# Expert queries one head at a time, the first head routed at once, later routings placed by the stream of gathered rows

## The chip, the cores and the metric

The kernel runs on one core of a Trainium2 chip (trn2). It was timed as device microseconds of whole executions: the median of three runs is 3098.87 us (3098.61 to 3099.56). The profile is of one further execution.

The engines are named as the profile has them: PE (TensorE, with PEld for its weight loads), DVE (VectorE), ACT (ScalarE), POOL (GpSimd) and SP (SyncE). Each runs its own instructions in order and waits for the others by semaphores. PE is TensorE's busy row, PEclk the clock granted to it, as a share of full speed.

## The reference

The model has two blocks of layers over 256 tokens of width 2048: a gated linear recurrence, attention with forget gates, and then a layer that mixes a recurrent branch with sparse attention. The change touches only the last part, a mixture of very many small experts. `x` has 256 rows; there are 8 heads, 128 x 128 experts and 16 experts per head and token.

```python
q = (xf @ wq).reshape(t, PEER_HEADS, PEER_QDIM)          # 256 columns per head
s1 = jnp.einsum('thd,kd->thk', q[..., :half], keys1)
s2 = jnp.einsum('thd,kd->thk', q[..., half:], keys2)
v1, i1 = lax.top_k(s1, PEER_TOPK)
v2, i2 = lax.top_k(s2, PEER_TOPK)
cand_s = (v1[..., :, None] + v2[..., None, :]).reshape(t, PEER_HEADS, -1)
cand_i = (i1[..., :, None] * PEER_KEYS + i2[..., None, :]).reshape(t, PEER_HEADS, -1)
top_s, pos = lax.top_k(cand_s, PEER_TOPK)
expert = jnp.take_along_axis(cand_i, pos, axis=-1).reshape(t, -1)
gate = jax.nn.softmax(top_s.astype(jnp.float32), axis=-1)
...
z = jnp.einsum('cd,ced->ce', xc, u[ec])
act = jax.nn.gelu(z, approximate=False) * gc
return jnp.einsum('ce,ced->cd', act, v[ec])
```

Each token reads 128 rows of `u` and 128 rows of `v`, each of 2048 float32. A residual sum and a final norm follow.

## The kernel before

**The weight loop.** All dense products go through one loop, `run`. It takes a list of steps; each step has 1024 columns per partition of weights (two steps are one load of 1 MB on SP's queue, into one of three `raw` buffers). The weights are split into a high part `hi` (a copy on ACT) and a low part `lo` (a subtraction on DVE), three steps ahead of PE, and PE multiplies 24 times per step. After the matmuls of a step the loop calls `pump`, which advances every open task by one piece, up to its next `yield`. So the order of instructions on each engine is fixed when the program is built: a task that yields lets the next step's `hi`, `lo` and matmuls go in between.

**The last 32 steps** make the experts' queries. Four units (`unit_B`, names `eq`) of 512 columns, that is two heads, have 8 steps each. When a unit ends, its task `e_query(n)` waits until the norm of the stream is known (`stE.done`; the row `stE_R` holds the factor of each token), scales the accumulator into `eq`, multiplies it with the two sets of keys on PE (`esc`), copies the scores (`es`), and calls `e_route` for token tile 0 and, when all four pairs have had theirs, for tile 1.

**Routing** (`e_route`) is DVE work: for two heads at once, four searches for the 16 highest of 128 scores (`top16`: MAX8, FIND_INDEX8, MATCH_REPLACE8, MAX8, FIND_INDEX8), 50 candidate pairs by nine additions and nine multiply-adds, a search over the 50 for each head, a comparison with a row of numbers to find the experts' numbers (three instructions over 128 x 800), a cast into `idx` (line 1349), and the softmax into `gate`. It yields some nine times.

**The stream** (`e_stream`) is a task too. It gathers rows: for each of 16 groups (8 heads x 2 token tiles) and each of 16 places, one gather of 128 rows from `e_u` (U) and one from `e_v` (V), 512 in all, each with an indirect DMA on POOL's queue (line 1363). U rows are multiplied with the token's row and summed on DVE (line 1393, 128 x 2048, "the product" below). V rows are scaled and summed on PE, as a matmul with a diagonal matrix `dg` (line 1411; ACT makes `dg`); in the last two groups every second V is added on DVE instead. Each piece of the task handles one row buffer and issues gathers for the free ones. There are three buffers (`rows_l`, and `rows_h` twice) until all queries are done; then `wide_rows` adds six (three `rows_w` in the place of `raw`, `rows_xh`, and `rows_xl` twice). U and V alternate once V may start, which is also when all queries are done.

In short, the DVE queue holds, in the order in which the tasks are advanced: `lo` of the weights, products of rows, pieces of routing, and query products.

Of the kernel before, what the change touches and what calls it, by code (L numbers as in the profile page):

```python
# [62 lines left out]
def tile_model(ctx: ExitStack, tc: tile.TileContext, x, xT, par, a_in, a_out, kv_in, kv_f, b_in, b_out,  # L63
# [313 lines left out]
    def unit_B(src, xt, cb, name, nk=KT):  # L377
# [850 lines left out]
    Ee = {"tk": 0, "r1": 0, "q": 0, "routed": [False] * NG16}  # L1228
# [24 lines left out]
    def e_query(n):  # L1253

        def f(acc):
            while not hasattr(stE, "done"):
                yield
            q = w4(f"eq{n}", (P, 4, T))
            tt_(q, acc, stE.R[:, None, :].to_broadcast([P, 4, T]), OP.mult)
            yield  # L1260
            yield
            ps = side_tile("esc").rearrange("p a (j k) -> p (a j) k", k=EK)
            for j in range(4):
                for t in range(TT):
# [17 lines left out]
            Ee["r1"] += 1  # L1282
# [18 lines left out]
    def e_route(n, tt, s):  # L1301

        NH = 2
        buf = w4(f"route{n}_{tt}")
        at = [0]

        def part(*shape):
# [3 lines left out]
            if len(shape) == 2:  # L1311
                return o.rearrange("p (a b) -> p a b", b=shape[1])
            return o.rearrange("p (a b c) -> p a b c", b=shape[1], c=shape[2])

        v, xi, ii = part(NH, 2, TK), part(NH, 2, TK), part(NH, 2, TK).bitcast(U32)
        cs, ci = part(NH, NCAND), part(NH, NCAND)
        tv, tp, pf, px = part(NH, TK), part(NH, TK).bitcast(U32), part(NH, TK), part(NH, TK)
        sm = part(NH, 1)
        for h in range(NH):
            for a_ in range(2):  # L1320
                top16(v[:, h, a_, :], ii[:, h, a_, :], s[:, (h * 2 + a_) * TT + tt, :])
            yield
# [13 lines left out]
        for r in range(NH):  # L1336
            top16(tv[:, r, :], tp[:, r, :], cs[:, r, :])
# [191 lines left out]
```

## Time and profile before

| what | value |
|---|---|
| median of three runs | 3098.87 us |
| the profiled execution, whole / its span | 3099.93 us / 3098.2 us |
| PE, DVE, ACT, POOL busy | 2677.9, 1912.0, 997.9, 780.9 us |
| queue of the gathers | 73728 packets, 536.90 MB |
| queue of the weights and other loads | 43920 packets, 298.73 MB |
| chain that ended last, by engine | PE 59%, DMA 25%, DVE 9%, issue 5%, POOL 2% |

The page gives the span in 40 slices of 77.5 us; there the bytes moved per slice and the busy shares of the engines show which stage runs. The first 22 slices are the dense layers, the gathers run from about slice 22 to the end. A share of busy time over the whole span mixes these stages, so the argument is made in the stage that the change touches.

### The profile page before, as it was taken

The page shows a single profiled execution, that of the slowest core. Times are in us where ns is not written, and L with a number is a line of the kernel's source. Part 1 is how long each engine was busy: PE and PEld are TensorE (multiplying, and loading weights), DVE is VectorE, ACT ScalarE, POOL GpSimd, SP SyncE. Part 2 cuts the span into 40 slices and gives each one's busy share as a digit, 9 for nine tenths or more (in the row PEclk, how much of TensorE's full clock was granted, in tenths as well). Part 3 has the DMA queues.
Part 4 walks back from the last instruction along what each step waited for, and adds up shares of the span by engine and source line. Part 5 has one row for each costly group of instructions (what it writes and reads, how often), then busy time and mean ns, then how long its engine had stood idle before and what let it go on. Part 6 is the DMA issues. An engine that isn't in the chain of part 4 may idle for free.

```text
span 3098.2 us, 34719 instructions
## 1 busy us (share of the span) xinstructions
PE 2677.9 (86%) x13236; PEld 1957.5 (63%) x13236; DVE 1912.0 (62%) x2840; ACT 997.9 (32%) x1545; POOL 780.9 (25%) x612
## 2 busy tenths in 40 slices
PE   8999999999999999999999747677777777777765
PEld 8999888888888899999989723222222222222222
DVE  7867665656665558566565899744444454444465
ACT  6545544555554445455454200100000000000000
POOL 0412110000000000000000143555555555554553
PEclk9999999999999999999999878899999999999988
DMA  7444445444445444444455689899999999999998
GB/s 260 150 149 151 167 160 178 164 162 177 167 154 193 175 164 171 161 173 170 171 177 192 231 316 358 358 421 422 421 422 421 421 422 422 421 421 422 422 421 332
DMA packets 118534, 841.13 MB, mean 271 GB/s; under 512 B 13152, under 2 KB 13536, under 8 KB 17376
## 3 DMA queue, kind: packets, MB, share of 16 engines
q0 software_dynamic: 73728, 536.90, 42.1%
q1 hardware_dynamic: 43920, 298.73, 27.0%
q10 hardware_dynamic: 720, 3.28, 0.3%
q8 instruction: 104, 1.70, 0.2%
q14 instruction: 62, 0.51, 0.0%
HBM read 836.77 MB, written 2.10 MB: 271 GB/s over the span
## 4 chain that ended last, share of the span: by engine, by line
PE 59%; DMA 25%; DVE 9%; issue 5%; POOL 2%; ACT 0%; POOLq 0%; DVEq 0%; ACTq 0%
DMA rows_w<-in_e_v_dram,slots 7%; DMA rows_xl<-in_e_v_dram,slots 5%; DMA rows_h<-in_e_v_dram,slots 5%; PE vacc L1411 5%; DMA rows_l<-in_e_v_dram,slots 3%; DMA rows_xh<-in_e_v_dram,slots 2%; DVE rows_h L1393 1%; PE S L554 1%; DVE eq L86 1%; PE aq L391 1%; PE aq L393 1%; PE aq L392 1%; PE az L391 1%; PE da L391 1%; PE az L392 1%
## 5 line engine op out<-in xcount | busy, mean ns | idle before, releaser
L86 DVE TENSOR_TENSOR lo<-raw,hi 128x1024 fp32r<-128x1024 f32 x424 | 520.3, 1232 | 301.7 <-PE dx L393 36.3
L102 ACT ACTIVATE hi<-raw 128x1024 fp32r<-128x1024 f32 x424 | 447.1, 1058 | 542.0 <-PE az L392 59.1
L1411 PE MATMUL vacc<-rows_w,dg_ring 128*128 128x512 f32 x640 | 311.3, 632 | 139.3 <-DMA rows_w<-in_e_v_dram,slots 93.2
L1411 PEld LDWEIGHTS vacc<-rows_w,dg_ring 128*128 128x128 f32 x640 | 122.3, 201 | 327.5 <-issue 211.0
L1411 PE MATMUL vacc<-rows_h,dg_ring 128*128 128x512 f32 x424 | 200.8, 619 | 82.9 <-DMA rows_h<-in_e_v_dram,slots 57.3
L1411 PE MATMUL vacc<-rows_xl,dg_ring 128*128 128x512 f32 x432 | 204.7, 618 | 69.5 <-DMA rows_xl<-in_e_v_dram,slots 62.6
L247 POOL TENSOR_TENSOR rq_y<-rq_m,mhalf 128x8 f32<-128x8 f32 (+2 forms) x24 | 31.6, 1317 | 888.2 <-DVE rq_m L95 881.6
L98 DVE SCALAR_TENSOR_TENSOR lo<-raw,prm,hi 128x512 fp32r<-128x512 f32 x256 | 178.8, 748 | 105.0 <-issue 62.0
L102 ACT ACTIVATE dg_ring<-ident,slots 128x128 f32<-128x128 f32 x240 | 83.6, 392 | 444.4 <-PE vacc L1411 444.2
L102 ACT ACTIVATE hi<-raw,prm 128x512 fp32r<-128x512 f32 x256 | 170.7, 717 | 120.8 <-PE bg L418 31.3
L1411 PEld LDWEIGHTS vacc<-rows_h,dg_ring 128*128 128x128 f32 x424 | 79.3, 196 | 203.6 <-issue 131.0
L1411 PEld LDWEIGHTS vacc<-rows_xl,dg_ring 128*128 128x128 f32 x432 | 80.8, 196 | 192.3 <-issue 145.2
L102 ACT ACTIVATE slots<-slots 128x16 f32<-128x16 f32 x16 | 3.4, 216 | 591.4 <-DVE rows_h L1393 142.9
L1393 DVE SCALAR_TENSOR_TENSOR rows_w<-rows_w,stE_r,rows_xh 128x2048 f32<-128x2048 f32 x43 | 101.1, 2351 | 106.4 <-DMA rows_w<-in_e_u_dram,slots 106.2
L1363 POOL DMA_INDIRECT rows_w<-in_e_u_dram,slots x80 | 125.9, 1574 | 155.8 <-PE vacc L1411 153.0
L1393 DVE SCALAR_TENSOR_TENSOR rows_w<-rows_w,stE_r,rows_l 128x2048 f32<-128x2048 f32 x37 | 86.9, 2349 | 74.7 <-DMA rows_w<-in_e_u_dram,slots 74.7
L1411 PE MATMUL vacc<-rows_l,dg_ring 128*128 128x512 f32 x208 | 98.2, 616 | 38.4 <-DMA rows_l<-in_e_v_dram,slots 26.1
L1411 PE MATMUL vacc<-rows_xh,dg_ring 128*128 128x512 f32 x216 | 101.8, 615 | 31.1 <-DMA rows_xh<-in_e_v_dram,slots 28.1
L1363 POOL DMA_INDIRECT rows_h<-in_e_u_dram,slots x64 | 95.1, 1485 | 132.5 <-PE vacc L1411 89.6
L1393 DVE SCALAR_TENSOR_TENSOR rows_xl<-rows_xl,stE_r,rows_xh 128x2048 f32<-128x2048 f32 x29 | 68.2, 2351 | 74.0 <-DMA rows_xl<-in_e_u_dram,slots 73.9
L1393 DVE SCALAR_TENSOR_TENSOR rows_h<-rows_h,stE_r,rows_l 128x2048 f32<-128x2048 f32 x36 | 84.5, 2347 | 46.6 <-DMA rows_h<-in_e_u_dram,slots 46.6
L1393 DVE SCALAR_TENSOR_TENSOR rows_h<-rows_h,stE_r,rows_xh 128x2048 f32<-128x2048 f32 x28 | 65.8, 2351 | 66.6 <-DMA rows_h<-in_e_u_dram,slots 66.5
(482 smaller groups left out, 7287.5 us busy)
## 6 DMA issues: line engine op xcount, KB each, us to landing
raw<-in_d_in_dram SPq DMA_DIRECT2D x76, 1024.0 KB, 4.8
raw<-in_a_in_dram SPq DMA_DIRECT2D x63, 1024.0 KB, 4.8
raw<-in_kv_in_dram SPq DMA_DIRECT2D x32, 1024.0 KB, 4.8
raw<-in_b_in_dram SPq DMA_DIRECT2D x32, 1024.0 KB, 4.7
raw<-in_a_out_dram SPq DMA_DIRECT2D x16, 1024.0 KB, 4.8
raw<-in_b_out_dram SPq DMA_DIRECT2D x16, 1024.0 KB, 4.8
raw<-in_d_out_dram SPq DMA_DIRECT2D x16, 1024.0 KB, 4.8
raw<-in_e_q_dram SPq DMA_DIRECT2D x16, 1024.0 KB, 4.8
```

Source lines behind the costliest of these rows:

```text
L86: V.tensor_tensor(o, a, b, op=op)
L98: V.scalar_tensor_tensor(o, a, s, b, op0=op0, op1=op1)
L102: S.activation(o, i, f, bias=bias, scale=scale)
L247: G.tensor_tensor(y, m, mhalf[:, :w], op=OP.pow)
L391: PE.matmul(a[:, j, :], lhsT=w_h, rhs=xt.h(kt), start=(kt == 0 and j % 2 == 0), stop=False)
L392: PE.matmul(a[:, j, :], lhsT=w_h, rhs=xt.l(kt), start=False, stop=False)
L393: PE.matmul(a[:, j, :], lhsT=w_l, rhs=xt.h(kt), start=False, stop=(kt == nk - 1 and j % 2 == 1))
L554: PE.matmul(o, lhsT=lhs[:, h, sl], rhs=r, start=True, stop=True)
L1363: G.indirect_dma_start(out=dst, out_offset=None, in_=table, in_offset=bass.IndirectOffsetOnAxis(ap=Ee["idx"][:, gi, k:k + 1], axis=0))
L1393: V.scalar_tensor_tensor(r, r, stE.r[:, t:t + 1], Ee["xw", t], op0=OP.mult, op1=OP.mult, accum_out=Ee["z"][:, gi, k:k + 1])
L1411: PE.matmul(accs[t][c // 2][:, c % 2, :], lhsT=dg, rhs=r[:, c * 512:(c + 1) * 512], start=(j == 0), stop=last)
```

## The change

Five things change, all in the experts' part.

- Units: 8 units of 256 columns (one head), 4 steps each, instead of 4 units of 512 columns with 8 steps (`unit_B2`). The weights are packed anew on the host; the steps, the matmuls and the bytes stay 32, 24 per step and 16 MB.
- The first head's query task has no `yield` between its product, its scores and its routing except one; the others keep theirs.
- `e_route` takes one head and one token tile. It has four pieces with a gap of a step between them. The searches are as before; the additions over the candidates have half the width, and as many instructions for one head as there were for two. The softmax takes its sum from ACT's exponential.
- A routing may start only when the ones ahead of it are done and the stream has issued U gathers to within 20 of its group's first one: `Ee["nu"]` is a count kept while the program is built.
- The scores of two heads share one tile `es`.

```diff
+        for i in range(4):
+            steps.append(Step(src(i // 2), mm(4 * i), ready=lambda k=i: xt.done() > k))
+        steps[-1].post = lambda: spawn(cb(box["acc"]))
...
-            q = w4(f"eq{n}", (P, 4, T))
-            tt_(q, acc, stE.R[:, None, :].to_broadcast([P, 4, T]), OP.mult)
-            yield
-            yield
-            ps = side_tile("esc").rearrange("p a (j k) -> p (a j) k", k=EK)
-            for j in range(4):
-                for t in range(TT):
...
+            q = w4(f"eq{h}", (P, 2, T))
+            tt_(q, acc, stE.R[:, None, :].to_broadcast([P, 2, T]), OP.mult)
+            yield
+            if h:
+                yield
+            ps = side_tile("esc")[:, 0, :].rearrange("p (t k) -> p t k", k=EK)
...
-            if Ee["q"] == 4:
+            if Ee["q"] == EH:
                 wide_rows()
-            yield
-            while Ee["tk"] < n:
-                yield
-            yield from e_route(n, 0, s)
-            Ee["tk"] += 1
-            while Ee["tk"] < 4 or Ee["r1"] < n:
-                yield
-            yield from e_route(n, 1, s)
-            Ee["r1"] += 1
+            for t in range(TT):
+                while Ee["route"] < t * EH + h or Ee["nu"] < (t * EH + h - 1) * TK - 4:
+                    yield
+                yield from e_route(h, t, s[:, 2 * t:2 * t + 2, :])
+                Ee["route"] += 1
...
+        for a_ in range(2):
+            top16(v[:, a_, :], ii[:, a_, :], s[:, a_, :])
+        yield
         V.tensor_copy(xi, ii)
...
+        top16(tv, tp, cs)
         V.tensor_copy(pf, tp)
...
+        V.tensor_reduce(px, eq, axis=AX.X, op=OP.add)
+        del eq
+        V.tensor_copy(Ee["idx"][:, gi, :], px)
+        Ee["routed"][gi] = True
+        yield
+        ts(tv, tv, tv[:, 0:1], OP.subtract)
+        act(tv, tv, AF.Exp, accum=sm)
+        yield
+        V.reciprocal(sm, sm)
+        ts(Ee["gate"][:, gi, :], tv, sm, OP.mult)
...
-                v_ok = Ee["q"] == 4 and nv < min(nu - nu % TK, len(us)) and \
+                v_ok = Ee["q"] == EH and nv < min(nu - nu % TK, len(us)) and \
...
                     it, nu = ("U",) + us[nu], nu + 1
+                    Ee["nu"] = nu
```

The order of instructions shows the change at three places. First ACT, from the row of the norm to the first scores; before, four `hi` copies of the steps after it stand between:

```order
L102 ACTIVATE hi_15225<-raw_15094 128x1024
L102 ACTIVATE stE_R<-Rps 128x256
L102 ACTIVATE hi_15258<-raw_15094 128x1024
L102 ACTIVATE hi_15288<-raw_15171 128x1024
L102 ACTIVATE hi_15319<-raw_15171 128x1024
L102 ACTIVATE hi_15356<-raw_15229 128x1024
L102 ACTIVATE es_15386<-esc 128x1024
```

Now one does, and the first `es` is half as wide:

```order
L102 ACTIVATE hi_15226<-raw_15094 128x1024
L102 ACTIVATE stE_R<-Rps 128x256
L102 ACTIVATE hi_15261<-raw_15094 128x1024
L102 ACTIVATE es_15294<-esc 128x512
L102 ACTIVATE hi_15309<-raw_15171 128x1024
L102 ACTIVATE hi_15365<-raw_15171 128x1024
```

So the first scores moved ahead by three weight steps of ACT's queue.

Second DVE, at the end of the first routing and the first products of rows (line 1393 before, 1410 now); `lo` are splits of weights. Before:

```order
L1345 TENSOR_REDUCE route_0_15416<-eq 128x16
L86 TENSOR_TENSOR lo_15626<-raw_15431,hi_15589 128x1024
L1349 CAST slots<-route_0_15416 128x32
L86 TENSOR_TENSOR lo_15664<-raw_15431,hi_15624 128x1024
L1393 SCALAR_TENSOR_TENSOR rows_l,slots<-rows_l,stE_r 128x2048
L1353 COPY route_0_15416<-route_0_15416 128x2
L86 TENSOR_TENSOR route_0_15416<-route_0_15416 128x32
L86 TENSOR_TENSOR lo_15703<-raw_15518,hi_15662 128x1024
L1393 SCALAR_TENSOR_TENSOR rows_h,slots<-rows_h,stE_r,rows_l 128x2048
```

Now, where the cast into `slots` follows its comparison at once:

```order
L1366 TENSOR_REDUCE route_0_15296<-eq 128x16
L1368 CAST slots<-route_0_15296 128x16
L86 TENSOR_TENSOR lo_15405<-raw_15171,hi_15365 128x1024
L1410 SCALAR_TENSOR_TENSOR rows_l,slots<-rows_l,stE_r 128x2048
L93 TENSOR_SCALAR route_0_15296<-route_0_15296 128x16
L86 TENSOR_TENSOR lo_15442<-raw_15230,hi_15403 128x1024
L1410 SCALAR_TENSOR_TENSOR rows_h,slots<-rows_h,stE_r,rows_l 128x2048
L1374 RECIPROCAL route_0_15296<-route_0_15296 128x1
```

Here the same sequence stands eight weight steps earlier: behind the first product 18 `lo` follow, before there were 10. Up to the first gather from `e_v` DVE has 25 products now and had 17.

Third POOL, where the first gather from `e_v` is issued and the buffers widen. Before, it is the 20th gather:

```order
L1363 DMA rows_l<-in_e_u_dram,slots 128x2048
L1363 DMA rows_h<-in_e_u_dram,slots 128x2048 x2
L1363 DMA rows_l<-in_e_u_dram,slots 128x2048
L1363 DMA rows_h<-in_e_v_dram,slots 128x2048
L1363 DMA rows_w_16244<-in_e_u_dram,slots 128x2048
L1363 DMA rows_w_16245<-in_e_v_dram,slots 128x2048
L1363 DMA rows_w_16246<-in_e_u_dram,slots 128x2048
```

Now it is the 28th, behind nine rounds of the three buffers:

```order
L1379 DMA rows_h<-in_e_u_dram,slots 128x2048 x2
L1379 DMA rows_l<-in_e_u_dram,slots 128x2048
L1379 DMA rows_h<-in_e_u_dram,slots 128x2048 x2
L1379 DMA rows_l<-in_e_v_dram,slots 128x2048
L1379 DMA rows_w_16224<-in_e_u_dram,slots 128x2048
L1379 DMA rows_w_16225<-in_e_v_dram,slots 128x2048
```

The order of U and V after that alternates in both; 19 V follow the last U before, 27 now. Behind the widening the routing of one head stands among 16 products each.

## Rows read from the trace of the kernel before

**Rows 1.** The page's slices of the span: GB/s in each of 40.

```profile
GB/s 260 150 149 151 167 160 178 164 162 177 167 154 193 175 164 171 161 173 170 171 177 192 231 316 358 358 421 422 421 422 421 421 422 422 421 421 422 422 421 332
```

**Rows 2.** Stretches: length, busy us of each engine, granted clock, DMA share, GB/s.

```profile
1720.00:1820.00 100.00, 55.64 (x381) 53.63 (x379) 90.11 (x212) 15.15 (x17) 22.93 (x20) 0.77 0.70 252
1820.00:2000.00 180.00, 119.74 (x240) 50.80 (x240) 164.05 (x475) 16.47 (x48) 85.30 (x66) 0.79 0.91 359
...
1840.00:1880.00 40.00, 29.63 (x63) 12.36 (x61) 38.52 (x133) 1.69 (x6) 18.75 (x15) 0.90 1.01 422
...
2000.00:3000.00 1000.00, 734.68 (x1578) 287.65 (x1576) 483.50 (x429) 72.16 (x214) 518.46 (x401) 0.99 1.01 422
3000.00:3080.00 80.00, 55.26 (x96) 21.42 (x96) 47.62 (x30) 3.98 (x11) 37.17 (x28) 0.83 1.00 415
```

**Rows 3.** Timeline of POOL (start, length, [idle before]): gathers 1, 20, 97, 512.

```profile
1725.52 1.21 POOL L1363 DMA_INDIRECT rows_l<-in_e_u_dram,slots  x1 [45.68 <-DVE slots L1349]
...
1819.31 1.45 POOL L1363 DMA_INDIRECT rows_h<-in_e_v_dram,slots  x1 [4.97 <-DVE rows_h L1393]
...
2024.03 1.66 POOL L1363 DMA_INDIRECT rows_xl<-in_e_u_dram,slots  x1 [2.06 <-PE vacc L1411]
...
3064.86 1.66 POOL L1363 DMA_INDIRECT rows_xl<-in_e_v_dram,slots  x1 [2.07 <-PE vacc L1411]
```

**Rows 4.** Timeline of ACT, DVE and PE: from the norm's row to the first scores.

```profile
1684.85 0.38 ACT L102 ACTIVATE stE_R<-Rps 128x256 f32<-128x256 f32 x1 [1.31 <-PE Rps L329]
...
1687.79 1.22 DVE L86 TENSOR_TENSOR eq<-eq,stE_R 128x1024 f32<-128x1024 f32 x1 [2.03 <-PE eq L393]
...
1693.28 1.95 PE L1265 MATMUL esc<-keys_iota,eq 128*128 128x128 f32 x16
...
1695.27 1.03 ACT L102 ACTIVATE es<-esc 128x1024 f32<-128x1024 f32 x1 [0.85 <-PE esc L1265]
```

**Rows 5.** Timeline of DVE: pieces of the first routing, of two heads.

```profile
1699.34 0.29 DVE L1295 MAX8 route<-es 128x8 f32<-128x128 f32 x1
...
1702.77 1.21 DVE L86 TENSOR_TENSOR lo<-raw,hi 128x1024 fp32r<-128x1024 f32 x1
...
1708.44 0.19 DVE L1323 CAST route<-route 128x64 f32<-128x64 uint32 x1
...
1710.02 1.22 DVE L86 TENSOR_TENSOR lo<-raw,hi 128x1024 fp32r<-128x1024 f32 x1
1711.15 0.21 DVE L1295 MAX8 route<-route 128x8 f32<-128x50 f32 x1
...
1713.78 1.21 DVE L86 TENSOR_TENSOR lo<-raw,hi 128x1024 fp32r<-128x1024 f32 x1
...
1715.11 0.99 DVE L86 TENSOR_TENSOR eq<-keys_iota,route 128x800 f32<-128x800 f32 x1
```

**Rows 6.** Timeline of DVE: the first products and what stands between them.

```profile
1733.10 2.35 DVE L1393 SCALAR_TENSOR_TENSOR rows_l<-rows_l,stE_r 128x2048 f32<-128x2048 f32 x1 [7.38 <-DMA rows_l<-in_e_u_dram,slots]
...
1735.37 0.17 DVE L1353 COPY route<-route 128x2 f32<-128x2 f32 x1
...
1735.68 1.22 DVE L86 TENSOR_TENSOR lo<-raw,hi 128x1024 fp32r<-128x1024 f32 x1
1736.82 2.35 DVE L1393 SCALAR_TENSOR_TENSOR rows_h<-rows_h,stE_r,rows_l 128x2048 f32<-128x2048 f32 x1
```

**Rows 7.** DMA issues: count, median us from issue to landing.

```profile
rows_w<-in_e_v_dram,slots POOLq DMA_INDIRECT x85, 18.8
...
rows_h<-in_e_u_dram,slots POOLq DMA_INDIRECT x64, 7.1
```

**Rows 8.** Waits of DVE from 2000 to 3080: us in total, times, longest.

```profile
DVE rows_w L1393 <- DMA rows_w<-in_e_u_dram,slots: 174.3, 66, 4.5
```

**Rows 9.** Timeline of DVE: the last V row.

```profile
3083.18 2.35 DVE L98 SCALAR_TENSOR_TENSOR xs<-rows_xl,slots,xs 128x2048 f32<-128x2048 f32 x1 [2.58 <-DMA rows_xl<-in_e_v_dram,slots]
```

**Rows 10.** Gathers of line 1363 from 2000: ns min/median/max, first and last start.

```profile
L1363 POOL DMA_INDIRECT rows_h<-in_e_v_dram,slots x50: 933/937/2806, 2007.4 to 3049.9; - x50
```

More of the change, by code (lines that the diff above doesn't have):

```diff
@@ L399, in unit_B, with unit_B2, mm, f @@
         steps[-1].post = lambda: spawn(cb(box["acc"].rearrange("p a (b t) -> p (a b) t", t=T)))
+        return steps
+    def unit_B2(src, xt, cb, name):
+        box = {}
+        steps = []
+        def mm(kt0):
+            def f(wh, wl):
+                if kt0 == 0:
+                    box["acc"] = acc_tile(name)[:, 0, :].rearrange("p (j t) -> p j t", t=T)
+                a = box["acc"]
+                h4, l4 = (w_.rearrange("p a (b n) -> p (a b) n", n=T) for w_ in (wh, wl))
+                for q in range(4):
+                    kt = kt0 + q
+                    for j in range(2):
+                        w_h, w_l = h4[:, q, j * P:(j + 1) * P], l4[:, q, j * P:(j + 1) * P]
+                        PE.matmul(a[:, j, :], lhsT=w_h, rhs=xt.h(kt), start=(kt == 0 and j == 0), stop=False)
+                        PE.matmul(a[:, j, :], lhsT=w_h, rhs=xt.l(kt), start=False, stop=False)
+                        PE.matmul(a[:, j, :], lhsT=w_l, rhs=xt.h(kt), start=False, stop=(kt == KT - 1 and j == 1))
+            return f
+        for i in range(4):
+            steps.append(Step(src(i // 2), mm(4 * i), ready=lambda k=i: xt.done() > k))
+        steps[-1].post = lambda: spawn(cb(box["acc"]))
         return steps
@@ L1227, in tile_model @@
     steps[-32].pre = lambda: spawn(resid_norm(stE, xD_done, xtE, "norm_ffn_g_2"))
-    Ee = {"tk": 0, "r1": 0, "q": 0, "routed": [False] * NG16}
+    Ee = {"q": 0, "route": 0, "nu": 0, "routed": [False] * NG16}
     rows = []
@@ L1251, in gain_rows, with e_query @@
         Ee["xw", t] = o
-    def e_query(n):
+    def e_query(h):
         def f(acc):
@@ L1310, in part @@
             at[0] += k
[L1311 to L1322, printed above, removed]
+            return o if len(shape) == 1 else o.rearrange("p (a b) -> p a b", b=shape[1])
+        v, xi, ii = part(2, TK), part(2, TK), part(2, TK).bitcast(U32)
+        cs, ci = part(NCAND), part(NCAND)
+        tv, tp, pf, px = part(TK), part(TK).bitcast(U32), part(TK), part(TK)
+        sm = part(1)
+        gi = tt * EH + h
+        for a_ in range(2):
+            top16(v[:, a_, :], ii[:, a_, :], s[:, a_, :])
+        yield
         V.tensor_copy(xi, ii)
@@ L1350, in e_route @@
-        for r in range(NH):
-            Ee["routed"][gi + r] = True
-        yield
-        V.tensor_copy(sm, tv[:, :, 0:1])
-        tt_(tv, tv, sm.to_broadcast([P, NH, TK]), OP.subtract)
-        act(tv, tv, AF.Exp)
-        yield
-        V.tensor_reduce(sm[:, :, 0], tv, axis=AX.X, op=OP.add)
-        V.reciprocal(sm[:, :, 0], sm[:, :, 0])
-        mul(Ee["gate"][:, gi:gi + NH, :], tv, sm.to_broadcast([P, NH, TK]))
+        eq = w4("eq", (P, TK, NCAND))
+        tt_(eq, Ee["iota"][:, None, :NCAND].to_broadcast([P, TK, NCAND]),
+            pf[:, :, None].to_broadcast([P, TK, NCAND]), OP.is_equal)
@@ L1443, in tile_model @@
     n0 = len(steps)
-    for n in range(4):
-        steps.extend(unit_B(lambda p, n=n: e_q[n, p], xtE, e_query(n), f"eq{n}"))
+    for h in range(EH):
+        steps.extend(unit_B2(lambda p, h=h: e_q[h, p], xtE, e_query(h), f"eq{h}"))
     steps[n0].pre = lambda: (spawn(e_setup()), spawn(e_stream()))
```

45 lines of the change are left out of this document (20 added, 25 removed).

## The prediction

> **What bounds the kernel now.** I read the slices of the whole span first, then stretches of it, then the engine that stands behind the slow stretch. The bytes per slice rise from some 170 GB/s to 422 from slice 26 on and stay there to the end [rows 1]. That tail is the stream of gathers: 512 of them, each 128 x 2048 x 4 bytes = 1.049 MB, so 1.049 MB / 422 GB/s = **2.485 us** apart when nothing else holds them. The stretches show where it isn't so: 252 GB/s from 1720 to 1820 us, 359 from 1820 to 2000, and 422 after that [rows 2]. In the first two VectorE is busy 90 of 100 and 164 of 180 us, in the third 484 of 1000: the stream is bound by VectorE until 2000 us and by the DMA engines from there. So the change can win only ahead of 2000 us, by an earlier start and by less VectorE work in front of the products of the gathered rows. It can win at most what the stream lacks there.
>
> The marks of the stream are four issues on GpSimd's queue [rows 3]: the first gather at 1725.52, the 20th (the first into the value table, when the buffers widen from three to nine) at 1819.31, the 97th at 2024.03, the 512th at 3064.86. From the 97th to the 512th there are 415 gathers in 1040.8 us, the saturated part; I leave that part as it is.
>
> **The change part by part, first gather.** Before, the first unit has 512 columns and 8 steps of TensorE; its product with the norm starts at 1687.79 [rows 4]. Two more steps, about 2.75 us each, pass until the scores (`esc`, 16 records) start at 1693.28; the copy `es` starts at 1695.27, and the first MAX8 at 1699.34 [rows 4, 5]. Now the unit has four steps and is long done, but it waits for the norm's row `stE_R`, which stands behind the 7th step: 1684.85 + 0.38 = 1685.2 [rows 4]. The half-size product ends at 1685.9; the scores stand behind the 8th step in TensorE's order, 1687.8; half the records take half of 1.95, to 1688.8, and half a copy 0.5; MAX8 at **1689.4**, 9.9 us sooner.
>
> The routing itself: before, two heads at once in pieces, one piece per step, from 1699.34 to the cast that the first gather waits for. Now one head, with its pieces joined: two searches over 128 scores 3.43 us (1699.34 to 1702.77), the pair sums at most 1.58 (1708.44 to 1710.02; half the width, but as many instructions), one search over 50 candidates half of 2.63 (1711.15 to 1713.78), the comparison three instructions of 0.99, the first at 1715.11 [rows 5], casts 0.4, and between them two weight splits of 1.14 (1735.68 to 1736.82) [rows 6] and a half-size query product 0.6. Sum 12.5, so 1701.9; the gather follows its cast within a microsecond, I allow 0.9: first gather at **1702.8** instead of 1725.5.
>
> **The stretch with three buffers.** VectorE stands still for the first rows, 7.6 us from the issue to the product [rows 3, 6]; TensorE runs dry for that long in both kernels, so this costs nothing new. The first product starts at 1710.4. From there the order gives VectorE's work until the 28th gather can be issued, which is now the one that goes to the value table: 25 products of 2.27 (1733.10 to 1735.37), 18 weight splits of 1.14, 6 query products of 0.6, two heads of routing and the rest of the first. A head costs 3.43 + 1.5 + 1.32 + 2.97 + casts 0.3 + its softmax 0.4, about 9.9 (the softmax from the same kind of rows, 0.31 us between 1735.37 and 1735.68 [rows 6], and as much again for the reciprocal and the scaling). Sum 56.8 + 20.5 + 3.6 + 19.8 + 0.8 = 101.5, so **1811.9**. The same sum on the kernel before (17 products, 10 splits, 2 full query products, almost two routings of two heads) gives 86.2, which from 1733.10 is 1819.3, where the 20th issue stands [rows 3, 6], so I trust the method.
>
> What the sum leaves out is waiting for rows. A buffer is free at the end of its product, and its next rows land 7.1 us after the issue [rows 7], with the issue some 0.4 later. With splits between the products VectorE is away 2 x 2.27 + 3 x 1.14 = 8.0 us, and needs no wait. For the last seven products there is no split left: one product each (7.5 + 2.27)/3 = 3.26 instead of 2.27, at most 7 us more, less the buffers that are full by then, about 5. So the 28th gather is issued between 1811.9 and 1819; I take **1814.5**.
>
> A rule bears on this wait: the Trainium skill, page "DMA: Bandwidth & Descriptors", section "Anatomy of one DMA — SWDGE (gpsimd) path", fits a single transfer as 2.0 us plus its bytes at 436 GB/s. For one gather that is an estimate of 4.4 us, and by it almost nothing waits and the 28th goes out at 1811.9, 3 us sooner than I take. The trace has 7.1 us for it and I go by that.
>
> **The stretch after it.** Before, the 20th gather has landed some 8 us after its issue (7.1 and a little for those right behind it), at 1827.3, and the 97th lands at 2024.03 + 18.8 = 2042.8 [rows 3, 7]: 77 gathers in 215.5 us, where 77 x 2.485 = 191.3 would do. The missing 24.2 us are the last five of the eight old routings, which follow each other without a pause. Now the count of issued gathers spreads them (it is counted when the program is written, so it sets an order and no engine waits on it): one head per 16 products, so per 32 gathers or 79.5 us VectorE has 16 x 2.27 + 9.9 = 46 us. In the saturated part it already waits 2.6 us for rows at each product (174.3 us in 66 waits) [rows 8], so a head finds room. A head's worst moment is two pieces, 6.4 us, between two products that are 4.97 us apart: 2.27 + 6.4 - 4.97 = 3.7 late, 4.3 after the third piece, made up at 2.6 per product. The queue covers it: rows land 18.8 us after their issue, against 7.1 with an idle queue, 11.7 us of cover [rows 7]. I take **no loss** for the 13 heads that are routed inside the stream. If the cover were gone they would cost up to 4.3 each.
>
> Some 12 us of VectorE work are added in all (16 heads at 9.9 against 8 pairs at some 18.3), in a stretch where half of VectorE is idle. ScalarE's extra copies and exponentials lie on an engine with 72 busy us in 1000 [rows 2]. TensorE's number of matmuls and the weight bytes stay the same. Values start 8 gathers later behind the products, so 27 instead of 19 values are left at the end; all of these are among the last two heads, where every second one is added by VectorE, and the tail stays on the DMA engines (415 GB/s there today, row of 3000 to 3080) [rows 2].
>
> **Sum.** The 28th lands at 1814.5 + 8 = 1822.5, the 97th 69 x 2.485 = 171.5 later, 1994.0, against 2042.8. That is **48.8 us** sooner: 24.7 until the buffers widen (8 gathers of 2.485, and 4.8 us) and 24.1 between there and the 97th. What follows is the same: the last rows at 3083.18 and 15 us of final norm [rows 9] move as a whole. The profiled execution took 3099.93 us, 1.06 above the median of the runs: 3051.1, and as a median **3050**.
>
> **The rivals.** (a) *Only the first half comes.* The old stretch after widening may lack bytes for another cause than the routings, say the start of the value products at the lower clock (granted 0.79 from 1820 to 2000 [rows 2], a mean of its two levels, 1.2 and 2.4 GHz). Against it: VectorE is the engine without idle time there. Gain 24.7, time 3074. Chance 0.10.
> (b) *TensorE bounds the query loop.* The clock granted from 1720 to 1820 is 0.77 [rows 2]. Were it at the lower level for all 18 steps, they would take 2 x 2.75 each, 99 us, then seven products: widening near 1827, 12 us later than I say, time 3062. For it: mean VectorE work per step is 4.7, close to 5.5. Chance 0.10.
> (c) *Slower: routing inside the saturated stream stalls it.* VectorE is 4.3 us late at each of 13 heads, and ScalarE's exponential, which waits for VectorE, stands ahead of the scalings of the next value rows, so buffers come free late and GpSimd's queue, in order, holds every gather behind them. It decides if the lateness isn't covered by the 11.7 us. Price 13 x 4.3 = 56 us, more than the whole gain: 3107. Against it: from 1840 to 1880, with VectorE busy 38.5 of 40 us, the old kernel still moves 422 GB/s [rows 2]. Chance 0.05.
> (d) *Issue becomes the bound.* An issue takes 0.94 us at the median and up to 2.81 [rows 10]; at 2.81 + 0.30 it would exceed 2.485. If the six gathers beside each head's routing were all that slow, 13 x 6 x 0.63 = 49 us are lost: 3100, no change. Chance 0.03.
> For (d) there is a rule: the Trainium skill, page "SBUF — State Buffer", section "SBUF: two separate sides", says that a VectorE instruction with two SBUF inputs and GpSimd take a shared port in turn, each for a whole instruction. By that rule the two comparisons of a head would each hold an issue for at most their own 0.99 us, which is less than the products do now.
>
> **How the numbers follow.** Forecast 0.72, (a) 0.10, (b) 0.10, (c) 0.05, (d) 0.03. The forecast's own bounds are 3046 to 3055 from the widening at 1811.9 to 1819. I take the range from 3040 (rows land sooner than 7.1 us and the heads overlap better) to 3070, which takes in (b) and leaves out (a), (c) and (d), 0.18. A change of 0.2%, some 6 us, is about what a measurement of this kernel tells from none. Faster: forecast, (a), (b), 0.92. Same: (d), 0.03. Slower: (c), 0.05.
>
> **What would show it.** The first gather near 1703 and the first product near 1710; the first gather into the value table as the 28th, near 1814; from 1830 on 422 GB/s in every stretch of 40 us; VectorE near 60% from there on, with idle time at each product; the issue to landing near 18.8 us all through. It is wrong if the three-buffer stretch ends after 1825, or if the bytes from 1830 to 2700 stay under 415 GB/s.

## The result

The changed kernel takes **3060.27 us** at the median (3060.12 to 3060.35, four runs), the kernel before 3098.74 on the same chip: a ratio of **0.9875**, interval 0.9858 to 0.9892. That is 38.5 us less, where 48.8 were forecast. The time lies in the range and the sign is as said, but a fifth of the gain is missing.

The slices of the whole span (page, second part) answer to [rows 1]: 421 GB/s is reached in slice 25, where it was slice 27 (the prediction reads slice 26 as full, but 25 and 26 stand at 358), and the two slices at 358 are gone.

```profile
GB/s 263 146 145 153 178 145 186 168 160 170 168 162 179 174 180 161 171 166 166 179 177 183 270 321 421 421 422 421 421 421 422 421 421 421 421 421 421 422 421 309
```

The same stretches as in [rows 2] (length, busy us of PE, PEld, DVE, ACT, POOL, granted clock, DMA share, GB/s), and two more with which the experiments are compared. From 1820 to 2000 the stream is saturated, 421 where it was 359, and VectorE (third pair) has 115 busy us in place of 164; from 1720 to 1820 it is still VectorE that is full, 93 of 100, but more of it is products, 300 GB/s in place of 252 (the last weight loads are in both).

```profile
1700.00:1820.00 120.00, 77.89 (x539) 75.88 (x538) 105.55 (x185) 24.50 (x34) 39.35 (x29) 0.79 0.80 297
1720.00:1820.00 100.00, 68.40 (x471) 66.59 (x469) 93.02 (x171) 19.61 (x27) 33.52 (x24) 0.81 0.81 300
1820.00:1900.00 80.00, 57.35 (x117) 23.50 (x118) 52.66 (x128) 7.51 (x19) 47.04 (x35) 0.86 1.01 421
1820.00:2000.00 180.00, 133.69 (x278) 54.08 (x279) 114.62 (x229) 18.83 (x49) 98.12 (x76) 0.92 1.01 421
1840.00:1880.00 40.00, 36.10 (x76) 14.97 (x76) 20.98 (x20) 6.49 (x15) 23.30 (x19) 0.93 1.01 422
2000.00:3000.00 1000.00, 741.71 (x1571) 293.31 (x1569) 576.80 (x934) 95.96 (x258) 504.86 (x399) 0.97 1.01 421
```

The marks of the stream on GpSimd's queue, as in [rows 3]: gathers 1, 20, then 26 to 28 (the 28th is now the first into the value table), 97 and 512.

```profile
1703.12 1.22 POOL L1379 DMA_INDIRECT rows_l<-in_e_u_dram,slots  x1 [22.73 <-DVE slots L1368]
...
1791.70 1.68 POOL L1379 DMA_INDIRECT rows_h<-in_e_u_dram,slots  x1 [2.95 <-DVE rows_h L1410]
...
1812.08 2.96 POOL L1379 DMA_INDIRECT rows_h<-in_e_u_dram,slots  x1 [1.94 <-DVE rows_h L1410]
1815.34 2.66 POOL L1379 DMA_INDIRECT rows_h<-in_e_u_dram,slots  x1 [0.30 <-issue]
1818.31 0.94 POOL L1379 DMA_INDIRECT rows_l<-in_e_v_dram,slots  x1 [0.30 <-DMA rows_xh<-in_f_g_dram]
...
1983.44 0.94 POOL L1379 DMA_INDIRECT rows_xl<-in_e_u_dram,slots  x1 [0.30 <-issue]
...
3025.39 1.67 POOL L1379 DMA_INDIRECT rows_h<-in_e_v_dram,slots  x1 [2.07 <-PE vacc L1428]
```

The first gather is 22.4 us sooner, the 20th 27.6, the 97th 40.6, the 512th 39.5. On VectorE, the first product, three of the last products ahead of the widening, the product of the 97th gather, and the last V row [rows 6, 9]:

```profile
1710.68 2.35 DVE L1410 SCALAR_TENSOR_TENSOR rows_l<-rows_l,stE_r 128x2048 f32<-128x2048 f32 x1 [7.36 <-DMA rows_l<-in_e_u_dram,slots]
...
1806.57 2.35 DVE L1410 SCALAR_TENSOR_TENSOR rows_l<-rows_l,stE_r 128x2048 f32<-128x2048 f32 x1 [3.19 <-DMA rows_l<-in_e_u_dram,slots]
...
1811.87 2.35 DVE L1410 SCALAR_TENSOR_TENSOR rows_h<-rows_h,stE_r,rows_l 128x2048 f32<-128x2048 f32 x1
...
1814.84 2.35 DVE L1410 SCALAR_TENSOR_TENSOR rows_l<-rows_l,stE_r 128x2048 f32<-128x2048 f32 x1 [0.61 <-DMA rows_l<-in_e_u_dram,slots]
...
1999.99 2.35 DVE L1410 SCALAR_TENSOR_TENSOR rows_xl<-rows_xl,stE_r,rows_l 128x2048 f32<-128x2048 f32 x1 [2.61 <-DMA rows_xl<-in_e_u_dram,slots]
...
3043.72 2.35 DVE L98 SCALAR_TENSOR_TENSOR xs<-rows_h,slots,xs 128x2048 f32<-128x2048 f32 x1 [2.60 <-DMA rows_h<-in_e_v_dram,slots]
```

### The profile page after: what moved, and what is told of

Its sections match the earlier page's. It is cut to its first block, busy times and chain, and to the rows that moved or that the text cites. A ratio compares the mean times of both kernels' runs of the same rounds, so it can differ in the third digit from the quotient of the medians.

```text
span 3058.6 us, 34945 instructions
## 1 busy us (share of the span) xinstructions
PE 2676.6 (88%) x13236; PEld 1959.9 (64%) x13236; DVE 1928.2 (63%) x3020; ACT 1022.8 (33%) x1595; POOL 774.1 (25%) x612
## 4 chain that ended last, share of the span: by engine, by line
PE 59%; DMA 26%; DVE 10%; issue 4%; POOL 1%; ACT 0%; DVEq 0%; POOLq 0%; ACTq 0%
DMA rows_w<-in_e_v_dram,slots 5%; DMA rows_h<-in_e_v_dram,slots 5%; PE vacc L1428 4%; DMA rows_xl<-in_e_v_dram,slots 3%; DMA rows_h<-in_e_u_dram,slots 3%; DMA rows_w<-in_e_u_dram,slots 3%; DMA rows_xl<-in_e_u_dram,slots 2%; DVE rows_h L1410 1%; PE S L579 1%; DMA rows_l<-in_e_v_dram,slots 1%; DMA rows_xh<-in_e_v_dram,slots 1%; DVE eq L86 1%; DVE rows_w L1410 1%; PE aq L391 1%; PE aq L393 1%
## 5 line engine op out<-in xcount | busy, mean ns | idle before, releaser
L1379 POOL DMA_INDIRECT rows_w<-in_e_u_dram,slots x77 | 116.7, 1516 | 138.8 <-PE vacc L1428 134.8
L1410 DVE SCALAR_TENSOR_TENSOR rows_h<-rows_h,stE_r,rows_l 128x2048 f32<-128x2048 f32 x40 | 93.8, 2348 | 43.1 <-DMA rows_h<-in_e_u_dram,slots 43.0
L1428 PEld LDWEIGHTS vacc<-rows_l,dg_ring 128*128 128x128 f32 x216 | 40.9, 199 | 108.8 <-issue 89.6
```

The lines of the kernel that those rows point to most:

```text
L1379: G.indirect_dma_start(out=dst, out_offset=None, in_=table, in_offset=bass.IndirectOffsetOnAxis(ap=Ee["idx"][:, gi, k:k + 1], axis=0))
L1410: V.scalar_tensor_tensor(r, r, stE.r[:, t:t + 1], Ee["xw", t], op0=OP.mult, op1=OP.mult, accum_out=Ee["z"][:, gi, k:k + 1])
L1428: PE.matmul(accs[t][c // 2][:, c % 2, :], lhsT=dg, rhs=r[:, c * 512:(c + 1) * 512], start=(j == 0), stop=last)
```

## The experiments

My theory: VectorE's work ahead of the widening, and routings that crowd behind it, bound the stream. The pacing (a routing waits for the count of issued gathers) takes both away, and a routing inside the saturated stream is free because rows lie in the queue. Rivals: the early first head is what gains; row waits or TensorE hold the first stretch; routing inside the stream costs its lateness.

The runs were taken on several chips, on which the kernel before had medians from 3098.7 to 3099.9 us. So medians in different rows are compared to about 1 us, no closer; the ratios are each to the kernel before on the same chip.

| run | edit | median us | ratio to before (interval) |
|---|---|---|---|
| changed kernel | | 3060.3 | 0.9875 (0.9858 to 0.9892) |
| e1_no_pacing | all but the pacing | 3108.1 | 1.0029 (1.0018 to 1.0040) |
| e3_before_paced | pacing, late pairs | 3065.8 | 0.9892 (0.9876 to 0.9909) |
| e2_head0_paced | first head like the others | 3060.8 | 0.9876 (0.9859 to 0.9892) |
| e4b_later12 | third head behind the widening | 3054.0 | 0.9854 (0.9838 to 0.9871) |
| e7_rows_early | weight buffers handed over early | 3057.4 | 0.9863 (0.9847 to 0.9880) |
| e8_both | the last two | **3050.7** | 0.9843 (0.9826 to 0.9859) |
| e12_spread | e8, pieces of routings set apart | 3051.1 | 0.9844 (0.9827 to 0.9860) |
| e10_before_late_rows | e3 with e8's two edits | 3059.8 | 0.9873 (0.9857 to 0.9890) |
| e5_compare_x2 | comparison twice | 3063.8 | 0.9883 (0.9867 to 0.9900) |
| e11_compare_x4 | four times | 3111.1 | 1.0035 (1.0025 to 1.0045) |
| e6_compare_x6 | six times | 3184.5 | 1.0270 (1.0253 to 1.0287) |
| e13_x6_spread | six times, products between | 3063.8 | 0.9883 (0.9867 to 0.9900) |

### Early head against pacing

The change has two parts, and two runs have one of them each. e1_no_pacing:

```diff
-while Ee["route"] < t * EH + h or Ee["nu"] < (t * EH + h - 1) * TK - 4:
+while Ee["route"] < t * EH + h:
```

> The changed kernel without the condition on the count of issued gathers: every routing starts as soon as the one before it is through. Theory (VectorE bounds the stream until the buffers widen, and routings are cheap only when they are spread): four routings and half a fifth stand ahead of the widening in place of two, 2.5 x 9.9 = 25 us of VectorE, so the first gather into the value table goes out near 1843 in place of 1818; behind it some ten routings follow each other with about four products each, 9.9 + 4 x 2.3 = 19 us per 8 gathers, which need 19.9, so little more is lost. Time 3083 to 3095. Rival (the early start alone makes the gain, pacing is idle): 3060, with the first value gather still near 1818.

It took 3108.1 us, above the 3083 to 3095 expected: without the pacing the rest of the change (the early head, single heads, small units) is no gain at all but a loss of 9 us. Three stretches and the first value gather of this run:

```profile
1700.00:1820.00 120.00, 76.05 (x525) 74.47 (x523) 109.80 (x271) 23.21 (x33) 25.62 (x23) 0.80 0.69 255
1820.00:1900.00 80.00, 38.65 (x76) 17.23 (x77) 76.76 (x244) 8.32 (x25) 39.03 (x29) 0.71 0.92 365
1900.00:2040.00 140.00, 94.26 (x191) 39.58 (x191) 122.58 (x404) 14.54 (x45) 56.19 (x47) 0.83 0.85 331
```

```profile
1839.34 1.44 POOL L1379 DMA_INDIRECT rows_l<-in_e_v_dram,slots  x1 [4.38 <-DVE rows_l L1410]
```

The 28th gather goes out 21.0 us later than in the changed kernel, about the 25 expected. But the crowd of routings behind it cost some 27 more (47.8 less 21.0), where I had allowed little. I had reckoned four products beside each routing. The trace has five products to two routings there, and so ten gathers to two heads. GpSimd's 56th and 86th issues show what that costs:

```profile
1914.44 0.94 POOL L1379 DMA_INDIRECT rows_w<-in_e_v_dram,slots  x1 [5.83 <-DVE route L93]
...
2011.82 0.94 POOL L1379 DMA_INDIRECT rows_xh<-in_e_v_dram,slots  x1 [6.43 <-DVE route L93]
```

Thirty gathers, with six heads routed beside them, take 97.4 us, and need 30 x 2.485 = 74.6. So 22.8 of the 27 us are lost in this part alone, at 3.8 for each head. VectorE's work says nearly the same: 2 x 9.9 + 5 x 2.27 = 31.2 us for ten gathers, which need 24.9.

e3_before_paced is the pacing alone, on the kernel before (the count `Ee["nu"]` is put in too):

```diff
-while Ee["tk"] < n:
+while Ee["tk"] < n or Ee["nu"] < (2 * n - 1) * TK - 4:
...
-while Ee["tk"] < 4 or Ee["r1"] < n:
+while Ee["tk"] < 4 or Ee["r1"] < n or Ee["nu"] < (EH + 2 * n - 1) * TK - 4:
```

> The kernel before (pairs of heads, units of 512 columns, first gather at 1725) with the pacing alone: a pair is routed when the count of issued gathers comes within 20 of it. Theory: ahead of the widening one and a half pairs fall away, some 13 to 20 us of VectorE less a few us of waits for rows, so the 20th gather goes out near 1804; behind it the 24 us of the crowded routings come back: 3060 to 3068, that is nearly all of the gain without the early first head. Rival (the start 22 us earlier is the main cause): 3080 or more.

3065.8 us, as the theory had it. The first gather stays late (1724.13 us), yet the 20th comes 15.5 us sooner than in [rows 3], and from 1820 on the stream is full:

```profile
1803.82 0.94 POOL L1363 DMA_INDIRECT rows_h<-in_e_v_dram,slots  x1 [1.89 <-DVE route L1353]
```

```profile
1700.00:1820.00 120.00, 77.29 (x541) 71.06 (x539) 103.70 (x214) 24.76 (x33) 38.61 (x28) 0.82 0.71 270
1820.00:1900.00 80.00, 59.81 (x129) 23.60 (x128) 37.47 (x34) 8.35 (x19) 43.00 (x35) 0.98 1.01 421
1900.00:2040.00 140.00, 105.06 (x227) 41.86 (x225) 83.74 (x139) 11.14 (x32) 73.12 (x56) 0.96 1.01 422
```

So of the 38.5 us the pacing alone brings 33.6 (3099.4 less 3065.8), and the whole rest of the change about 5. Without pacing that rest is worth minus 9.

e2_head0_paced takes out the two shortcuts of the first head:

```diff
-if h:
-    yield
+yield
```

(at both places of the query step).

> The changed kernel with the two shortcuts of the first head taken out: its scores and their copy each wait one more step, as those of the other heads do. Theory: first gather some 5.5 us later, near 1708.5, the buffers still widen near 1819, but the first value gather is the 26th, not the 28th, so two gathers (5.0 us) are missing at the point from which the stream is saturated: 3064 to 3067. Rival (the start is hidden behind something else, such as TensorE's steps): 3060 within 1.

A miss: 3060.8, no change, as the rival had it, but not for the rival's reason. Its first gather, and its first value gather, the 26th:

```profile
1705.34 1.81 POOL L1377 DMA_INDIRECT rows_l<-in_e_u_dram,slots  x1 [24.87 <-DVE eq L86]
...
1812.99 0.93 POOL L1377 DMA_INDIRECT rows_h<-in_e_v_dram,slots  x1 [1.67 <-DVE rows_h L1408]
```

I had the start 5.5 us later and the widening at the same time. It started only 2.2 later (why not 5.5 I did not trace), and with two products fewer ahead of it the widening came 5.3 us sooner, which is just the two gathers missing (2 x 2.485 = 5.0). While VectorE bounds the stretch, a product that is done earlier only moves the widening by its own length: the sum of VectorE's work counts, not the moment of the first gather.

### What bounds the stretch with three buffers

e4b_later12 moves one routing out of it, by the threshold alone (the later routings start 16 gathers later too):

```diff
-... Ee["nu"] < (t * EH + h - 1) * TK - 4:
+... Ee["nu"] < (t * EH + h - 1) * TK + 12 * (t * EH + h > 1):
```

> The changed kernel with a later threshold: the third head is routed behind the widening and not ahead of it, the later ones 16 gathers later than now. Theory (VectorE's work bounds the stretch with three buffers): 9.9 us of VectorE fall away there, less 3 to 5 us of new waits for rows, so the first value gather goes out at 1811 to 1814 and the time is 3052 to 3056. Rival (waits for rows, or TensorE at its lower clock, already end last in that stretch): the value gather stays at 1816 to 1818, time 3058 to 3061.

3054.0 us, 6.3 less than the changed kernel. The 28th gather:

```profile
1811.09 3.04 POOL L1379 DMA_INDIRECT rows_l<-in_e_v_dram,slots  x1 [0.30 <-DMA rows_xh<-in_f_g_dram]
```

7.2 us sooner for 9.9 us of VectorE: VectorE was the bound, and 2.7 come back. The stretch from the start of the first product to the end of the 25th, first of the changed kernel and then of this run, shows as what:

```profile
1710.68:1817.19 106.51, 70.82 (x480) 69.01 (x480) 101.05 (x180) 24.50 (x34) 34.06 (x24) 0.79 0.82 303
```

```profile
1709.68:1809.98 100.30, 67.04 (x480) 65.73 (x480) 91.79 (x129) 24.30 (x32) 33.23 (x24) 0.81 0.86 324
```

VectorE has 9.3 us less work and is idle 8.5 us in place of 5.5; what is added are waits for rows. TensorE is not the bound: the same 480 matmuls pass in 6.2 us less, at nearly the same granted clock.

e7_rows_early gives the stream the three row buffers that are former weight buffers as their last weights are split (the routings from the fourth head on start 4 gathers later by it, so that they stay behind the widening):

```diff
...
+for i in range(NRAW):
+    steps[len(steps) - 2 * NRAW + 1 + 2 * i - LOOK_SPLIT].pre = lambda i=i: early_row(i)
```

> The changed kernel with the three row buffers that are former weight buffers handed to the stream one by one as their last weights are split (9, 7 and 5 steps of TensorE before the end) and not all at the last query; the third and later heads keep their places behind the widening. Theory (in the last 20 to 25 us before the widening three buffers hold the stream at some 305 of 422 GB/s): up to 7 us of stream come back, 3053 to 3057, the first value gather is the 32nd. Rival (GpSimd's issues of up to 3 us beside the products, or VectorE, hold it): 3059 to 3061.

3057.4, a gain of 2.9 where 3 to 7 were expected. So waits for rows held a part of the stretch too. Two stretches say where most of the rest went:

```profile
1700.00:1820.00 120.00, 77.65 (x537) 75.95 (x535) 107.01 (x186) 24.20 (x33) 49.48 (x34) 0.79 0.85 326
1820.00:1900.00 80.00, 52.06 (x110) 21.18 (x111) 54.90 (x102) 8.14 (x20) 47.07 (x32) 0.84 0.98 403
```

Up to 1820 it moves 326 GB/s where the changed kernel has 297, 120 x 29 / 422 = 8.2 us of stream. But behind the widening it moves 403 where that has 421: 80 x 18 / 422 = 3.4 us are given back, in the stretch where the fourth head is routed while the queue has only begun to fill. What became of the other 1.9 is not shown.

e8_both has both edits, the third head again by a later threshold (so have the heads behind it, except the ninth):

```diff
-... Ee["nu"] < (t * EH + h - 1) * TK - 4:
+... Ee["nu"] < (t * EH + h - 1) * TK + 16 * (t + h > 1):
```

> Early row buffers together with the third head behind the widening and the later thresholds. Theory (VectorE's work and the three buffers each hold a part of the stretch): below both single edits, 3046 to 3051. Rival (both take away the same waits): 3053 to 3055.

It takes **3050.7 us**, the shortest of all (e12 below is the same within the noise): 9.6 below the changed kernel, about the sum of the two (6.3 + 2.9). It too gives some back behind the widening:

```profile
1820.00:1900.00 80.00, 58.94 (x128) 24.46 (x128) 50.49 (x101) 8.94 (x22) 46.99 (x34) 0.90 0.97 398
```

e10_before_late_rows does the same to the kernel before, so with a first gather at 1725.75 and pairs of heads. Beside the early row buffers, against e3:

```diff
-... Ee["nu"] < (2 * n - 1) * TK - 4:
+... Ee["nu"] < (2 * n - 1) * TK + 8:
...
-... Ee["nu"] < (EH + 2 * n - 1) * TK - 4:
+... Ee["nu"] < (EH + 2 * n - 1) * TK + 7:
```

> The kernel before, with pairs of heads and its late first gather, with the pacing, the second pair behind the widening of the buffers, and the row buffers from the weights handed over early. Theory (VectorE's work ahead of the widening and the pacing decide, the moment of the first gather does not): 18.3 us of VectorE less than with the pacing alone, less some 5 us of waits for rows: 3048 to 3056. Rival (a start 22 us later can't be made up once VectorE is no longer the bound): 3062 to 3066.

3059.8: neither the theory's range nor the rival's. Its stretches ahead of 1820 and behind it, and e8_both's ahead of 1820:

```profile
1700.00:1820.00 120.00, 77.35 (x547) 72.83 (x545) 102.91 (x213) 22.53 (x24) 43.95 (x31) 0.82 0.82 324
1820.00:1900.00 80.00, 58.44 (x127) 24.31 (x128) 46.68 (x48) 9.21 (x26) 44.05 (x34) 0.90 0.91 363
```

```profile
1700.00:1820.00 120.00, 73.55 (x528) 71.51 (x527) 103.44 (x152) 23.93 (x31) 50.20 (x35) 0.78 0.90 351
```

363 GB/s, so 80 x 59 / 422 = 11.2 us are lost there, 6.6 more than in e8_both. My reading is that a pair of heads is twice as long a piece. At 1820 it is behind already: 324 GB/s against 351 is 7.7 us (the last weight loads are in both). The two make more than the 9.1 us between the runs, so some is won back later; no run parts the later start from the pairs. So single heads and an early start are worth 5 us with the pacing alone, and 9 once VectorE's load ahead of the widening is down.

### What a routing costs inside the saturated stream

Three runs repeat the comparison block, in each of the 13 heads from the fourth on:

```diff
+for _ in range(N if gi >= 3 else 0):
+    tt_(eq, ...is_equal); tt_(eq, eq, ci..., OP.mult); V.tensor_reduce(px, eq, ...)
```

with N = 1, 3 and 5 (2.97 us of VectorE each), for the block twice (e5), four times (e11) and six times (e6).

> The changed kernel with the comparison block (three instructions, 2.97 us of VectorE) done twice in each of the 13 heads that are routed inside the saturated stream. Theory (a late product is covered by the 11.7 us that rows lie in the queue): the worst lateness grows from 4.3 to some 7.3 us, still under the cover, so nothing is lost: 3060 to 3063. Rival (routing stalls the stream by its lateness): 13 x 3 = 39 us more, 3099.

> The same with the block done six times in place of once, 14.9 us more of VectorE in each of the 13 heads, in one piece. Theory (cover of 11.7 us): VectorE is some 16 us late at each head, 4.5 more than the cover, so 13 x 4.5 = 58 us are lost and the bytes dip at each head: 3105 to 3130. Rival 1 (only VectorE's sum counts, 61 us of work per 79.5 us of stream): 3060 to 3063. Rival 2 (no cover at all): 13 x 14.9 = 194 us, 3254.

> The changed kernel with the comparison block four times in place of once in each of the 13 heads (8.9 us more of VectorE in one piece; twice gave 3063.8, six times 3184.5). In the trace with six times GpSimd waits 18.2 us at each head and a head takes 90.7 us in place of 79.5: the queue covered some 7 us, not 11.7. Theory with a cover of 7 us: GpSimd waits some 12.3 us, 5.2 are lost at each head, 13 x 5.2 = 68 us, 3115 to 3130. Rival (cover of 11.7, as I had it): 3060 to 3075.

Medians 3063.8 (twice), 3111.1 (four times; scattered, 3100 to 3118) and 3184.5 (six times). All three lie outside what the theory gave: 0.8 us above 3063, 3.9 below 3115, and 54.5 above 3130. The view to read is GpSimd's timeline: the longest idle time ahead of an issue, which comes back at every head. One of the changed kernel:

```profile
1902.19 1.44 POOL L1379 DMA_INDIRECT rows_l<-in_e_v_dram,slots  x1 [4.09 <-DVE rows_l L1410]
```

With the block twice, then two in a row with it four times, and two with it six times:

```profile
1912.97 0.94 POOL L1384 DMA_INDIRECT rows_w<-in_e_v_dram,slots  x1 [5.95 <-DVE route L1379]
```

```profile
2007.73 0.94 POOL L1384 DMA_INDIRECT rows_h<-in_e_v_dram,slots  x1 [12.09 <-DVE route L1379]
...
2093.19 0.94 POOL L1384 DMA_INDIRECT rows_w<-in_e_v_dram,slots  x1 [12.09 <-DVE route L1379]
```

```profile
2204.66 0.94 POOL L1384 DMA_INDIRECT rows_h<-in_e_v_dram,slots  x1 [18.23 <-DVE route L1379]
...
2295.33 0.94 POOL L1384 DMA_INDIRECT rows_xh<-in_e_v_dram,slots  x1 [18.23 <-DVE route L1379]
```

GpSimd stands still 4.1, 5.95, 12.1 and 18.2 us. A pause of 2.1 us stands between pairs of issues even where nothing is routed ([rows 3]). The loss against the changed kernel is 0.3, 3.9 and 9.6 us per head (3.5, 50.8 and 124.2 over 13). So a stall of some **8 us** is covered (12.1 less 3.9 is 8.2, 18.2 less 9.6 is 8.6), and what lies above is paid in full. The cover exists, but it is less than the 11.7 us that I read from the landing times. The changed kernel's 4.1 lie well under it, so its 13 heads are free, as I said: from 2000 to 3000 it moves 421 GB/s with routings in it, and the kernel before, which has none there, 422 [rows 2].

e13_x6_spread has the block six times too, with a product between each two:

```diff
+    yield
+    yield
     tt_(eq, ...is_equal) ...
```

> The block six times as before (14.9 us more of VectorE in each head), but with one product of VectorE between each two blocks in place of none. Theory (what costs is the longest stay away from the products, not the sum of the work): no stay is longer than in the changed kernel, 3060 to 3066. Rival (the sum of the work costs): as with one piece, 3150 to 3190.

3063.8 us, against 3184.5 in one piece, with the same work on VectorE. GpSimd's stall at a head is back at that of the changed kernel:

```profile
2062.66 1.45 POOL L1386 DMA_INDIRECT rows_w<-in_e_v_dram,slots  x1 [4.08 <-DVE rows_w L1417]
```

So it is the longest stay away from the products that costs, and hardly the sum. A little is left for the sum, in the long stretch:

```profile
2000.00:3000.00 1000.00, 744.41 (x1566) 297.79 (x1564) 722.84 (x1096) 102.64 (x261) 511.28 (x398) 0.95 1.01 418
```

418 GB/s against 421 is 7 us, of which some come back at the end of the stream (last section).

e12_spread sets the pieces of each later head apart in e8_both:

```diff
     top16(v[:, a_, :], ii[:, a_, :], s[:, a_, :])
+    if gi > 2 and not a_:
+        yield
+        yield
```

and one more step behind the searches and behind the pair sums; the routings from the fourth on start at 4 gathers past (gi - 1) * 16.

> The kernel with the third head behind the widening and early row buffers (3050.7), and from the fourth head on the three pieces of a routing set a product apart, one search at a time. Theory (what is left in the saturated stretch is lost at the routings' long pieces): the 1 to 3 us by which its bytes lie under 422 GB/s come back, 3047 to 3050. Rival (the longest piece is covered already): 3050 to 3051.

No gain, 3051.1 (the rival's 3050 to 3051): once under the cover, shorter pieces bring nothing. The 421 GB/s of that stretch stay as they are.

## Why the prediction was right, and where it was off

**What bounds the kernel, and where the gain can lie**: right. The stream was not saturated until 2000 us because of VectorE: with 49 busy us of VectorE gone between 1820 and 2000 it is saturated from 1820 on, and e3 has the same by the pacing alone.

**First gather and first product**: 1702.8 and 1710.4 forecast, 1703.12 and 1710.68 measured. The step sum held in its parts too: the first MAX8 starts at 1689.59 (1689.4 forecast), the cast at 1702.01 (1701.9).

**The stretch with three buffers** holds the term that was mis-sized. VectorE's sum led to 1811.9, and I added 2.6 us of the up to 7 that waits for rows could cost: 1814.5. It was 1818.31, so 6.4 of the 7. The sum of the work itself was right: 101.05 busy us from the first product to the end of the 25th (e4b's rows above), 101.5 forecast. What was too small is the wait. Two things are seen in the rows above: VectorE waits 3.19 us for the rows of 1806.57 and 0.61 for those of 1814.84, and the 26th and 27th issue take 2.96 and 2.66 us in place of 0.94, so the 27th is through at 1818.00, after the last product (1814.84 + 2.35 = 1817.19) has set its buffer free. I had put long issues under rival (d), in the saturated stretch, where they cost nothing; they came where products of VectorE follow each other with hardly a pause. On the rule that I weighed for this wait, the estimate of 4.4 us from the Trainium skill, page "DMA: Bandwidth & Descriptors", section "Anatomy of one DMA — SWDGE (gpsimd) path": the trace disagrees again. The first gather takes 7.6 us from its issue to its product.

**From the widening to the 97th**: I had the 28th land 8 us after its issue, at 1822.5. Its matmul starts at 1827.32, 9.0 after the issue:

```profile
1827.32 6.08 PE L1428 MATMUL vacc<-rows_l,dg_ring 128*128 128x512 f32 x8 [15.65 <-DMA rows_l<-in_e_v_dram,slots]
```

To the 97th (taken at 1999.99 by its product) there are 172.7 us, forecast 171.5. So the 97th is 6.0 us later than forecast: 3.8 from the issue, 1.0 from the landing, 1.2 on the way. Against before, where its product stands at 2043.09, it is 43.1 us sooner:

```profile
2043.09 2.35 DVE L1393 SCALAR_TENSOR_TENSOR rows_xl<-rows_xl,stE_r,rows_l 128x2048 f32<-128x2048 f32 x1 [2.61 <-DMA rows_xl<-in_e_u_dram,slots]
```

"422 GB/s in every stretch of 40 us" held: 419 to 423.

**No loss at the 13 heads**: right, shown by e5, e11, e6 and e13. The reason was right as a kind, its size wrong: 8 us, not 11.7. The lateness forecast, 4.3 us, lies under that cover too, so "up to 4.3 each" never came due.

**"What follows is the same"**: not quite. Of the 43.1 us at the 97th, 39.5 are left at the last V row, so 3.6 were given back. The 13 routings have no loss to show for it: from 2000 to 3000 the two kernels move 421 and 422 GB/s, which is at most some 2.4 us. What the trace has is the end of the stream (below); no run parts it.

**The split of the gain** was misleading. I had 24.7 us until the widening and 24.1 behind it, and the working of the first began with a first gather 22.7 sooner. By the issues and products 20.9 and 22.2 came. But by the runs with one part each it is the pacing that makes both halves; the rest of the change without it loses 9 us, and a start 2.2 us later changes nothing (e2).

**The rivals**: (a) fell, since the second half came. (b) would have given 3062, and the time of 3060 looks like it; the range took both in and could not have told them apart. e4b shows that it was VectorE: 9.9 us of its work gone brought the 28th gather 7.2 us sooner with TensorE's steps unchanged. (c) does exist as a mechanism: at six blocks it makes the kernel slower by 2.7%. Here it stays below its point. (d) had no part in the saturated stretch, which stayed at 421 GB/s.

Added up: 48.8 forecast, less 3.8, 1.0 and 1.2 ahead of the 97th and 3.6 behind it, is 39.2; the profiled spans differ by 39.6 (3098.2 and 3058.6), the medians by 38.5.

## What to carry to other kernels

When one engine both prepares a stream's addresses and consumes its rows, put the preparation just in time: done ahead it delays the stream's ramp, done in a crowd it starves it, and done one piece at a time in the saturated part it is free, as long as no piece keeps the engine away for longer than the queued rows last (here some 8 us). Look for the bound of the ramp by that engine's whole sum up to the point where the buffers widen; an earlier first transfer gains little while that sum stays.

## What the hardware showed that was not expected

**The stream ends slowly.** The bytes per slice in the last 14 us up to the last V row, of the changed kernel, of the one before, and of e13_x6_spread (40 slices of 0.35 us each):

```profile
GB/s 421 398 398 445 421 445 421 421 421 421 304 304 281 328 257 234 234 164 94 94 47 47 47 47 23 23 23 47 23 23 23 23 23 23 47 23 23 0 0 0
```

```profile
GB/s 375 445 445 468 421 375 398 445 375 445 468 445 421 375 421 421 398 421 468 445 398 328 304 328 328 257 281 234 187 187 140 70 47 47 70 23 23 0 0 0
```

```profile
GB/s 421 398 398 398 468 421 445 421 421 398 398 398 468 421 445 421 421 398 421 375 468 421 445 421 421 375 375 281 328 187 94 94 23 23 23 23 47 0 0 0
```

In the changed kernel the bytes fall from 3033.5 on, 10.2 us ahead of the last V row, and for some 6 us they run at 23 to 47 GB/s, about what one or two of 16 engines carry (421 / 16 = 26). Before, they fell 6.2 us ahead of it, 4 us later. My reading is that the last rows are there only when the slowest engine has done its share, while the others idle; this fits the 3.6 us that were given back. In e13, with the same end of the program, the fall is some 5 us ahead of the end, so it is not a matter of the code at the end. What sets how far the engines drift apart stays open.

The Trainium skill, page "DMA: Bandwidth & Descriptors", section "Latency and other measured facts", names two of the 16 engines as usually slower than the rest in traces. By that rule one or two would be the last to end; the number agrees with the 23 to 47 GB/s here. Which engines they are no view here shows.

**The length of a gather's issue**: 0.94 us by itself, 2.7 to 3.0 for the two issues that begin just behind the start of a product (1812.08 and 1815.34 above). Both end 0.8 us after that product does: 1812.08 + 2.96 = 1815.04, and the product ends at 1811.87 + 2.35 = 1814.22; 1815.34 + 2.66 = 1818.00, and the product ends at 1817.19. In the whole trace of the changed kernel 242 of the 512 issues begin while such a product, or another operation of VectorE on two tiles of 0.9 us and more, is running. 226 of them end 0.81 us after it does, within 0.03; the other 270 take 0.93 to 0.96 us. So an issue that comes while a product runs is held until that product is through, up to some 2 us; what the two share no run here shows.
